# Queries and keys of heads 0 and 1 as two pairs of seven products ahead of the attention, parked in DRAM

## The chip, the cores and the metric

One core of a Trainium2 chip runs the kernel. The metric is device time in microseconds (us) of one execution. The kernel before was timed three times: 1097.13, 1096.53 and 1094.05 us, median 1096.53.

Every engine of the core runs its own instructions in its own order: TensorE (PE) multiplies, VectorE (DVE) and ScalarE (ACT) do elementwise work, GpSimd (POOL) and SyncE (SP) issue DMAs, and GpSimd also adds.

## What is computed

One block over 1024 tokens of width 1024. An adaLN-modulated RMSNorm gives `h`; one wide product `h @ w_in` gives everything else. The part that matters here is the gated linear attention:

```
q, k, v, z_gla, ra_f, ra_b, u, vs, z_gmlp, m_gla, m_gmlp = split(h @ w_in)
log_a = maximum(log_sigmoid(ra @ alpha_w + alpha_b) / 16, -1.25)      # per direction
b = cumsum(log_a) within chunks of 64 tokens
q_t, k_t, k_end = q * exp(b), k * exp(-b), k * exp(b_last - b)
attn = where(mask, q_t @ k_t.T, 0)
state = exp(b_last) * state + k_end.T @ v          # from chunk to chunk
o = attn @ v + q_t @ state                         # forward and backward, added
y_gla = (rmsnorm_per_head(o) * gla_norm_g * silu(z_gla)) @ w_br_gla
y_gmlp = (gelu(u) * spatial_gate(vs) * silu(z_gmlp)) @ w_br_gmlp
out = rmsnorm(x + gate * ((sigmoid(m_gla)*y_gla + sigmoid(m_gmlp)*y_gmlp) @ w_out))
```

There are 4 heads; a head's query and key have 128 columns each, its value 256.

## The kernel before

**Products.** Every fp32 matrix is split into a high part (rounded to fp32r) and a low part (the rest): `split_w` (L171) casts on ScalarE and subtracts on VectorE. One product of two matrices is then three matmuls: high by high, high by low, low by high. All activations lie with channels on partitions.

**Two ways to a block of columns.** A block is 128 columns of `w_in` over 1024 tokens.
- *Dense*: `dense_fm` (L185) and `fm_half` (L965) run 2 halves of 512 tokens by 8 slices of the inner dimension by 3 matmuls, 48 matmuls of 128x512 for a block.
- *Pair*: `pair` (L602) computes two blocks at once by seven products instead of eight, each `prod` (L580) of 12 matmuls of 128x512, 84 for two blocks where dense takes 96. It needs sums of the weights, which GpSimd makes (L610, L611, L612, L617), and sums of the results, which VectorE makes (L629 to L643), and it works on sums of `h` (`TS`) that are held while the pairs run.

**Stages.** First `h`, the values of heads 0 and 1 and the spatial gate. Then the pairs, one after another: `pair_m` (tanh of the merge gates, to DRAM), `pair_uz` (gMLP), `pair_z` (the gate of the attention, to DRAM `z_d`); the last is `pair_z(3)`. Around the end of the pairs stands `dense_q(0)`, and the transposes `low_rank` (L767) that make `RT`, the input of the decays.

**Attention.** 16 units (4 heads by 4: backward halves 1 and 0, forward halves 0 and 1). In `gla_unit` a *decay chain* runs for one unit: the decay product on TensorE (L793), Abs, Exp and Ln on ScalarE, two steps and a scan on VectorE, two Exp, and the products with `q` and `k`, of which `b` (L821) is the last. Then the *scores* (L830) can start. `front_a` of unit n+2 is emitted behind `front_b` (scores) of unit n+1, so that the decay product of the next unit directly follows the scores of this one on TensorE. Between the attention's small matmuls stands a *filler*: the list `jobs`, a generator that gives out dense work in steps of 12 matmuls of 128x512 (or 24 of 128x256 for values). `QUOTA` says how many steps are emitted per unit. The jobs before are key of head 0, query and key of head 1, value of head 2, query and key of head 2, value of head 3, query and key of head 3, and the blocks of `y_gmlp` (operand `gg`, loaded from DRAM by `load_gg`).

**End.** The last filler blocks, the product with `w_br_gla` (operand `GO`, loaded as `gf` from `g_d` and split to `gh`, `gl`), and the output projection.

**Order.** Each engine runs its instructions in the order in which the scheduler of the framework has put them, with a simulated timeline in mind; it moves instructions of independent work past each other within the limits of the buffers. SyncE's queue holds the weight loads. GpSimd's queue holds the DRAM writes of the pairs and the loads of `v`, `z` and, on a changed kernel, of `q` and `k`.

Of the kernel before, what the change touches and what calls it, by code (L numbers as in the profile page):

```python
# [9 lines left out]
F32 = mybir.dt.float32  # L10
F32R = mybir.dt.float32r
I8 = mybir.dt.int8
AF = mybir.ActivationFunctionType
ALU = mybir.AluOpType
# [3 lines left out]
P = 128  # L18
D = 1024
T = 1024  # L20
KC = D // P
NT = T // P
# [9 lines left out]
FB_Q, FB_K, FB_Z, FB_U, FB_ZG, FB_MA, FB_MB, FB_YA, FB_YB = 0, 4, 8, 16, 24, 32, 40, 48, 56  # L32
# [12 lines left out]
def hybrid_block_kernel(ctx: ExitStack, tc: tile.TileContext, x, wf, wt, wada, wgate, wvr, wst, alpha, abias,  # L45
                        pcols, prows, out):
    nc = tc.nc
    V, S, G, TE = nc.vector, nc.scalar, nc.gpsimd, nc.tensor
# [17 lines left out]
    def dram(name, shape, dtype=F32):  # L66
        return dr.tile(shape, dtype, tag=name, name=name)
# [6 lines left out]
    tb_d = dram("tb_d", [KC, P, T])  # L74
    z_d = dram("z_d", [KC, P, T])
    gate_d = dram("gate_d", [2, 512])
    b12_d = dram("b12_d", [4, P, 1024])

    v_d = [dram(f"v{n}_d", [HEADS, 2, P, 4 * 256]) for n in "hl"]
# [11 lines left out]
    def pm():  # L91
        return ps.tile([P, 512], F32, tag="m", bufs=2, name=nm("pm"))

    def po_():
        return ps.tile([P, 512], F32, tag="o", bufs=2, name=nm("po"))
# [5 lines left out]
    ident = cp.tile([P, P], F32, name="ident")  # L101
# [7 lines left out]
    ones = cp.tile([P, P], F32, name="ones")  # L109
# [5 lines left out]
    ra = cp.tile([P, NT, 32], F32, name="ra")  # L115


    def ht(shape, dtype, name):
        return hp.tile(shape, dtype, tag="h", bufs=30, name=nm(name))

    def w4(shape, dtype, name):
        return hp.tile(shape, dtype, tag="w", bufs=13, name=nm(name))

    def w2(shape, dtype, name):
        return hp.tile(shape, dtype, tag="s", bufs=18, name=nm(name))
# [32 lines left out]
    H = Act("h")  # L158
# [26 lines left out]
    def dense_fm(b, x, evac):  # L185

        hi, lo = fm_weights(b)
        for half in range(2):
            acc = pd()
            for k in range(KC):  # L190
                TE.matmul(acc, lhsT=hi[:, k, :], rhs=x.hi(k, half), start=(k == 0), stop=False)
                TE.matmul(acc, lhsT=hi[:, k, :], rhs=x.lo(k, half), start=False, stop=False)
                TE.matmul(acc, lhsT=lo[:, k, :], rhs=x.hi(k, half), start=False, stop=(k == KC - 1))
            evac(half, acc)
# [43 lines left out]
    for b in range(2):  # L238
        pc = pd()
        sl = slice(b * 512, b * 512 + 512)  # L240
# [307 lines left out]
    TOKENS = (4, 5, 6, 7, 0, 1, 2, 3)  # L548
# [11 lines left out]
    def v_weights(h, new):  # L560
        pieces = []
        for j in range(2):
            w = stage(wt[WV + 2 * (h - 1) + j])
            hi, lo = new([P, 4, HV], F32R, "tvh"), new([P, 4, HV], F32R, "tvl")
            split_w(w, flat(hi), flat(lo))
            for k in range(4):
                pieces.append((hi[:, k, :], lo[:, k, :]))
        return pieces
# [77 lines left out]
    def pair_m(b0, d, i):  # L646

        def ev(b, half, acc):
            m = w2([P, 512], F32, "m")
            S.activation(m, acc, AF.Tanh, scale=0.5)  # L650
            G.dma_start(d[2 * i + b, :, half * 512:half * 512 + 512], m)
        pair(b0 + 2 * i, b0 + 2 * i + 1, ev)
# [22 lines left out]
    def pair_z(i):  # L675

        def ev(b, half, acc):
            z = w2([P, 512], F32, "z")
            last_tanh[0] = S.activation(z, acc, AF.Tanh, scale=0.5)
            V.scalar_tensor_tensor(out=z, in0=z, scalar=1.0, in1=acc, op0=ALU.add, op1=ALU.mult)  # L680
            G.dma_start(z_d[2 * i + b, :, half * 512:half * 512 + 512], z)
        pair(FB_Z + 2 * i, FB_Z + 2 * i + 1, ev)

    last_tanh = [None]

    def low_rank_weights():

        ST = w4([P, T], F32R, "ST")
        sa, sr = ht([P, 1024], F32, "sa"), ht([P, 1024], F32R, "sr")
        G.memset(sa, 0.0)  # L690
        for r in range(3):
            G.dma_start(sa[r * 32:r * 32 + 16, 0:512], alpha[0])
            G.dma_start(sa[r * 32 + 16:r * 32 + 32, 512:1024], alpha[1])
        G.dma_start(sa[96:98, :], abias.partition_broadcast(2))
        S.copy(sr, sa)
        S.copy(ST[0:64, :], sr[0:64, :].bitcast(F32))
        V.tensor_tensor(out=sa[64:128, :], in0=sa[64:128, :], in1=sr[64:128, :].bitcast(F32), op=ALU.subtract)
        S.copy(ST[64:96, :], sa[64:96, :])
        S.activation(sa[96:128, :], sa[96:128, :], AF.Copy, scale=ident[96:128, 97:98])
        V.scalar_tensor_tensor(out=ST[96:128, :], in0=sr[96:128, :].bitcast(F32), scalar=ident[96:128, 96:97],  # L700
                               in1=sa[96:128, :], op0=ALU.mult, op1=ALU.add)
        return ST

    pair_m(FB_MB, tb_d, 0)
    pair_m(FB_MB, tb_d, 1)
    pair_uz(0)
# [8 lines left out]
    pair_m(FB_MA, ta_d, 2)  # L715
    pair_z(1)
    pair_m(FB_MA, ta_d, 3)
    pair_z(2)
    ST = low_rank_weights()
    pair_z(3)  # L720

    with tc.issue_after(last_tanh[0].ins):
# [8 lines left out]
    q_t = [None] * HEADS  # L731
    k_t = [None] * HEADS
    z_t = [[None, None] for _ in range(HEADS)]

    def dense_q(h):
        q_t[h] = ht([P, T], F32, "q")

        def ev(half, acc):
            S.activation(q_t[h][:, half * 512:half * 512 + 512], acc, AF.Copy, scale=float(P) ** -0.5)
        dense_fm(FB_Q + h, H, ev)  # L740

    def dense_k(h):
        k_t[h] = ht([P, T], F32, "k")

        def ev(half, acc):
            S.copy(k_t[h][:, half * 512:half * 512 + 512], acc)
        dense_fm(FB_K + h, H, ev)

    def load_z(h):
        for j in range(2):  # L750
            zt = z_t[h][j] = ht([P, T], F32, "zg")
            G.dma_start(zt, z_d[2 * h + j])

    RT = w4([P, T], F32R, "RT")

    V.tensor_copy(RT[96:128, :].rearrange("p (a b) -> p a b", b=P), ones[96:128].unsqueeze(1).broadcast_to([32, 8, P]))


    r3 = ht([P, NT, 3, 32], F32, "r3")
    for t in range(NT):  # L760
        V.tensor_copy(r3[:, t], ra[:, t, :].unsqueeze(1).broadcast_to([P, 3, 32]))

    def low_rank(half):
        sl = slice(half * 512, half * 512 + 512)
        pr = po_()
        for i in range(4):
            TE.transpose(pr[0:96, i * P:(i + 1) * P], r3[:, half * 4 + i].rearrange("p a b -> p (a b)"), ident)  # L767
        S.copy(RT[0:96, sl], pr[0:96])
        V.tensor_tensor(out=RT[32:64, sl], in0=pr[32:64], in1=RT[32:64, sl].bitcast(F32), op=ALU.subtract)

    v_t = {}

# [6 lines left out]
    V.memset(smask, 1.0)  # L779
    V.memset(smask.rearrange("p (c k) -> p c k", k=C)[:, :, 0:1], 0.0)  # L780

    dense_q(0)
    low_rank(1)
    low_rank(0)
    load_v(0, 1)
    load_v(0, 0)

# [189 lines left out]
    def ev_q(h):  # L977
        def ev(half, acc):
            S.activation(q_t[h][:, half * 512:half * 512 + 512], acc, AF.Copy, scale=float(P) ** -0.5)
        return ev  # L980

    def ev_k(h):
        def ev(half, acc):
            S.copy(k_t[h][:, half * 512:half * 512 + 512], acc)
        return ev
# [10 lines left out]
    def prep_qk(h, isk):  # L996
        (k_t if isk else q_t)[h] = ht([P, T], F32, "qk")
        return fm_weights((FB_K if isk else FB_Q) + h)

    def run_fm(x, evac, halves=(1, 0)):  # L1000
        def run(w):
            for half in halves:
                yield from fm_half(x, w, half, evac)
        return run

    def run_v(h):
        def run(pieces):
            for t in TOKENS:
                acc = pd()[:, 0:HV]
                v_steps(acc, pieces, t)  # L1010
                v_out(h, t, acc)
                yield
        return run
# [24 lines left out]
    def gg_second():  # L1038
        load_gg(1)
        return held["yb"]  # L1040

    jobs = [(lambda: prep_qk(0, True), run_fm(H, ev_k(0))),
            (lambda: prep_qk(1, False), run_fm(H, ev_q(1))),
            (lambda: prep_qk(1, True), run_fm(H, ev_k(1))),
            (lambda: v_weights(2, w4), run_v(2)),
            (lambda: prep_qk(2, False), run_fm(H, ev_q(2))),
            (lambda: prep_qk(2, True), run_fm(H, ev_k(2))),
            (lambda: v_weights(3, w4), run_v(3)),
# [23 lines left out]

    order = [(h, u) for h in range(HEADS) for u in range(4)]

    QUOTA = (4,) * 14 + (3, 3)
    load_z(0)
    dense(4)
    front_a(*order[0])
# [6 lines left out]
    for n, (h, u) in enumerate(order):  # L1085
        nxt = order[n + 1] if n + 1 < len(order) else None
        if u == 0 and h > 0:
            load_z(h)
        if u == 3 and h + 1 < HEADS:
            load_v(h + 1, 0)  # L1090
        if u == 1 and h + 1 < HEADS:
            load_v(h + 1, 1)
        last = order[n - 1] if n and SEQ[order[n - 1][1]][0] else None
        if last:
            norm(*last)
        dense(1)
        step(h, u, 0)
        dense(1)
        if last:
            output(*last)  # L1100
        step(h, u, 1)
        dense(QUOTA[n] - 3)
        if nxt:
            front_b(*nxt)
        step(h, u, 2)
        if n + 2 < len(order):
            front_a(*order[n + 2])
        dense(1)
        step(h, u, 3)
        if nxt:  # L1110
            front_c(*nxt)
# [226 lines left out]
```

## Time and profile before

| | us |
|---|---|
| median of three runs | 1096.53 |
| profiled execution | 1096.96 |
| its span | 1095.3 |
| outside the span | 1.7 |
| TensorE busy | 1057.6 |
| VectorE busy | 641.1 |
| ScalarE busy | 412.1 |
| GpSimd busy | 276.1 |

A row of the timeline gives start, busy time, engine, line, operation and, in brackets, the idle time before it with what ended it. Matmuls are pipelined: a 128x512 matmul is shown as 0.39 to 0.40 us long, while the next one starts earlier; its cost to the engine is the distance of starts. In windows the columns are the stretch, its length, and busy us (with the number of instructions) of PE, PEld, DVE, ACT and POOL; then the clock granted to TensorE as a share of full speed, the share of the DMA engines that was busy, and GB/s. A row of the waits gives who waited for whom, us in total, times, longest.

### The profile page before, as it was taken

Reading aid. Unit: us, or ns where it says so; the run is one execution under the profiler, and the core shown is the slowest. Engines: PE = TensorE matmul, PEld = TensorE weight load, DVE = VectorE, ACT = ScalarE, POOL = GpSimd, SP = SyncE. Lnnn points to the kernel's source line nnn. Section 1 sums busy time; section 2 is a strip of 40 time slices with the busy share of each in tenths; the row PEclk is TensorE's granted clock in tenths of the full one; section 3 lists DMA queues with packets and bytes.
Section 4 is the critical chain, followed back from the end, with each engine's and each line's share of the span. In section 5 each row is a group of like instructions: output and inputs, shape, how many; then the busy total and the mean of one; then the engine's idle time right before and its main releaser. Section 6 shows DMA issues by size and latency. Waiting matters only on the chain.

```text
span 1095.3 us, 14011 instructions
## 1 busy us (share of the span) xinstructions
PE 1057.6 (97%) x5292; PEld 892.7 (82%) x5292; DVE 641.1 (59%) x960; ACT 412.1 (38%) x721; POOL 276.1 (25%) x304
## 2 busy tenths in 40 slices
PE   6899999999999999999999999999999989995997
PEld 4688899888888888878888898998888778884886
DVE  5777497346547464664554576658767556345522
ACT  4454334233333323343323546457254253111322
POOL 2311203424334352453402001102011010005510
PEclk9899999999999999999999999999999999997999
DMA  9532276233233323223348024347344385235012
GB/s 362 215 128 70 104 253 221 79 118 104 106 116 106 125 97 119 103 104 135 135 145 291 17 83 149 131 140 250 128 161 136 127 294 183 83 119 193 1 58 96
DMA packets 57032, 152.80 MB, mean 140 GB/s; under 512 B 7457, under 2 KB 15649, under 8 KB 56966
## 3 DMA queue, kind: packets, MB, share of 16 engines
q1 hardware_dynamic: 42198, 102.42, 27.0%
q0 software_dynamic: 14768, 49.50, 12.5%
q8 instruction: 41, 0.67, 0.3%
q14 instruction: 25, 0.20, 0.1%
HBM read 108.90 MB, written 43.00 MB: 139 GB/s over the span
## 4 chain that ended last, share of the span: by engine, by line
PE 81%; DVE 5%; issue 5%; DMA 4%; ACT 2%; POOL 1%; SPq 0%; POOLq 0%; ACTq 0%; DVEq 0%
PE pd L210 5%; PE pd L211 5%; PE po L589 4%; PE po L587 4%; PE po L588 4%; PE pd L209 4%; PE pd L969 4%; PE pd L970 4%; PE pd L971 4%; PE pk L587 3%; PE pk L589 3%; PE pk L588 3%; PE pd L587 3%; PE pd L588 3%; PE pd L589 3%
## 5 line engine op out<-in xcount | busy, mean ns | idle before, releaser
L543 PE MATMUL pd<-tvh,hh 128*128 128x256 f32 (+1 forms) x256 | 75.0, 293 | 0.0
L544 PE MATMUL pd<-tvl,hh 128*128 128x256 f32 (+1 forms) x256 | 73.8, 288 | 0.0
L545 PE MATMUL pd<-tvh,hl 128*128 128x256 f32 (+1 forms) x256 | 73.4, 287 | 0.0
L219 POOL TENSOR_TENSOR r<-ms,nhalf 128x1 f32<-128x1 f32 (+1 forms) x24 | 21.6, 900 | 193.1 <-DVE ms L218 184.5
L589 PE MATMUL pd<-hh,al 128*128 128x512 f32 x160 | 62.5, 390 | 0.0
L587 PE MATMUL pd<-hh,ah 128*128 128x512 f32 x160 | 62.3, 390 | 0.0
L588 PE MATMUL pd<-hl,ah 128*128 128x512 f32 x160 | 62.3, 389 | 0.0
L209 PE MATMUL pd<-th,mh 128*128 128x512 f32 x120 | 47.0, 403 | 7.8 <-ACT th L173 7.8
L969 PE MATMUL pd<-ggh,wh 128*128 128x512 f32 x128 | 51.8, 405 | 1.8 <-ACT wh L173 1.8
L210 PE MATMUL pd<-tl,mh 128*128 128x512 f32 x120 | 48.3, 403 | 3.5 <-DVE tl L174 3.5
L971 PE MATMUL pd<-ggh,wl 128*128 128x512 f32 x128 | 51.6, 405 | 0.0
L970 PE MATMUL pd<-ggl,wh 128*128 128x512 f32 x128 | 51.1, 399 | 0.0
L174 DVE TENSOR_TENSOR al<-wa,ah 128x1024 fp32r<-128x1024 f32 x20 | 31.4, 1571 | 32.7 <-PE po L588 30.8
L1167 PE MATMUL pd<-gl,wh 128*128 128x512 f32 x128 | 49.8, 389 | 0.0
L1166 PE MATMUL pd<-gh,wl 128*128 128x512 f32 x128 | 49.6, 389 | 0.0
L1165 PE MATMUL pd<-gh,wh 128*128 128x512 f32 x128 | 49.6, 389 | 0.0
L610 POOL TENSOR_TENSOR wsum<-wb 128x512 f32<-128x512 f32 x20 | 25.8, 1288 | 94.2 <-DMA wb<-in_wf 69.7
L544 PEld LDWEIGHTS pd<-tvl,hh 128*128 128x128 f32 x256 | 48.7, 190 | 0.9 <-issue 0.5
L543 PEld LDWEIGHTS pd<-tvh,hh 128*128 128x128 f32 x256 | 48.7, 190 | 0.8 <-issue 0.5
L545 PEld LDWEIGHTS pd<-tvh,hl 128*128 128x128 f32 x256 | 48.7, 190 | 0.0
L211 PE MATMUL pd<-th,ml 128*128 128x512 f32 x120 | 48.0, 400 | 0.0
L174 DVE TENSOR_TENSOR wl<-ws,wh 128x1024 fp32r<-128x1024 f32 x24 | 29.3, 1220 | 30.0 <-ACT wh L173 28.8
(318 smaller groups left out, 3108.0 us busy)
## 6 DMA issues: line engine op xcount, KB each, us to landing
ws<-in_wf SPq DMA_DIRECT2D x24, 512.0 KB, 5.3
ws<-in_wt SPq DMA_DIRECT2D x22, 512.0 KB, 4.8
wa<-in_wf SPq DMA_DIRECT2D x20, 512.0 KB, 3.6
wb<-in_wf SPq DMA_DIRECT2D x20, 512.0 KB, 4.6
wa<-in_wada SPq DMA_DIRECT2D x16, 512.0 KB, 9.3
xn<-in_x SPq DMA_DIRECT2D x8, 512.0 KB, 7.4
sg_d<-sg POOLq DMA_DIRECT2D x16, 256.0 KB, 3.1
wg<-in_wgate SPq DMA_DIRECT2D x16, 256.0 KB, 5.3
```

What stands on the lines that cost most here:

```text
L209: TE.matmul(acc, lhsT=xh, rhs=hi[:, k % 2, :], start=(k == 0), stop=False)
L210: TE.matmul(acc, lhsT=xh, rhs=lo[:, k % 2, :], start=False, stop=False)
L211: return TE.matmul(acc, lhsT=xl, rhs=hi[:, k % 2, :], start=False, stop=(k == KC - 1))
L543: TE.matmul(acc, lhsT=H.hi_t(k, t), rhs=hi, start=(k == 0), stop=False)
L544: TE.matmul(acc, lhsT=H.hi_t(k, t), rhs=lo, start=False, stop=False)
L545: i = TE.matmul(acc, lhsT=H.lo_t(k, t), rhs=hi, start=False, stop=(k == KC - 1))
L587: TE.matmul(acc, lhsT=a, rhs=xh(k), start=(first and k == 0), stop=False, skip_group_check=not first)
L588: TE.matmul(acc, lhsT=a, rhs=xl(k), start=False, stop=False, skip_group_check=not first)
L589: TE.matmul(acc, lhsT=b, rhs=xh(k), start=False, stop=(k == 3), skip_group_check=not first)
L969: TE.matmul(acc, lhsT=hi, rhs=x.hi(k, half), start=(k == 0), stop=False)
L970: TE.matmul(acc, lhsT=hi, rhs=x.lo(k, half), start=False, stop=False)
L971: TE.matmul(acc, lhsT=lo, rhs=x.hi(k, half), start=False, stop=(k == KC - 1))
```

## The change

`q` and `k` of heads 0 and 1 are no longer computed densely. Two new pairs, over blocks `FB_Q`, `FB_Q+1` and `FB_K`, `FB_K+1`, compute them among the other pairs and write them to new DRAM tensors `q_d` and `k_d`. `load_qk(h)` brings them back by GpSimd's queue, head 0 ahead of the attention and head 1 in its second unit. The transposes for `RT` move ahead of `pair_z(3)` and use another PSUM buffer. The first three filler jobs are gone, so the list opens with the values of head 2, and the quota falls from 62 to 52 steps.

```diff
+    def pair_qk(b0, d, scale):
+        def ev(b, half, acc):
+            r = w2([P, 512], F32, "z")
+            S.activation(r, acc, AF.Copy, scale=scale)
+            G.dma_start(d[b, :, half * 512:half * 512 + 512], r)
+        pair(b0, b0 + 1, ev)
...
     pair_m(FB_MA, ta_d, 3)
+    pair_qk(FB_Q, q_d, float(P) ** -0.5)
     pair_z(2)
     ST = low_rank_weights()
+    pair_qk(FB_K, k_d, 1.0)
+    RT = w4([P, T], F32R, "RT")
+    low_rank_inputs(RT)
     pair_z(3)
...
-    def dense_q(h):
-    def dense_k(h):
...
+    def load_qk(h):
+        for l, d in ((q_t, q_d), (k_t, k_d)):
+            l[h] = ht([P, T], F32, "qk")
+            for half in (1, 0):
+                sl = slice(half * 512, half * 512 + 512)
+                G.dma_start(l[h][:, sl], d[h, :, sl])
...
-    dense_q(0)
-    low_rank(1)
-    low_rank(0)
+    load_qk(0)
...
-    jobs = [(lambda: prep_qk(0, True), run_fm(H, ev_k(0))),
-            (lambda: prep_qk(1, False), run_fm(H, ev_q(1))),
-            (lambda: prep_qk(1, True), run_fm(H, ev_k(1))),
-            (lambda: v_weights(2, w4), run_v(2)),
+    jobs = [(lambda: v_weights(2, w4), run_v(2, (0, 1, 2, 3, 4, 5, 6, 7))),
...
-    QUOTA = (4,) * 14 + (3, 3)
+    QUOTA = (3, 3, 4, 3) * 4
...
+        if (h, u) == (0, 1):
+            load_qk(1)
```

`low_rank_inputs` holds the lines of the old `low_rank`, with `pm()` in place of `po_()`.

On TensorE the end of the pairs is, before, the last product of `pair_z(3)` (L587 to L589), the last matmuls of head 0's query (L191 to L193), the transposes (L767) and the key of head 0 (L969 to L971):

```order
L589 MATMUL pk_4537<-hh_106,fl_4474 128x512
L193 MATMUL pd_4645<-hh_106,wl_4616 128x512
L191 MATMUL pd_4645<-hh_106,wh_4615 128x512
L192 MATMUL pd_4645<-hl_107,wh_4615 128x512
L193 MATMUL pd_4645<-hh_106,wl_4616 128x512
L767 MATMUL po_4671<-ident,r_800_4600 96x128 x4
L969 MATMUL pd_4704<-hh_4590,wh_4700 128x512
```

After, head 2's values (L545 to L547, 128x256) stand between the products of `pair_z(3)` (L589 to L591) on TensorE:

```order
L547 MATMUL pd_4962<-tvh_4914,hl_99 128x256
L545 MATMUL pd_4962<-tvh_4914,hh_98 128x256
L546 MATMUL pd_4962<-tvl_4915,hh_98 128x256
L547 MATMUL pd_4962<-tvh_4914,hl_99 128x256
L589 MATMUL pk_4830<-t0h_1539,sh_4757 128x512
L590 MATMUL pk_4830<-t0l_1540,sh_4757 128x512
L591 MATMUL pk_4830<-t0h_1539,sl_4758 128x512
```

The dense query and the transposes have left this place, and the filler now begins among the pairs.

In head 3, the unit of TensorE that ends with the scores of the first forward half closes before like this; `ggh`, `ggl` with L969 to L971 are filler, L848 to L850 state products, L830 the next scores:

```order
L848 MATMUL pk_7145<-vh_6550,keh_7045 128x256
L849 MATMUL pk_7145<-vl_6551,keh_7045 128x256
L850 MATMUL pk_7145<-vh_6550,kel_7046 128x256
L969 MATMUL pd_7251<-ggh_6581,wh_7076 128x512
L970 MATMUL pd_7251<-ggl_6582,wh_7076 128x512
L971 MATMUL pd_7251<-ggh_6581,wl_7077 128x512
...
L969 MATMUL pd_7251<-ggh_6588,wh_7076 128x512
L970 MATMUL pd_7251<-ggl_6589,wh_7076 128x512
L971 MATMUL pd_7251<-ggh_6588,wl_7077 128x512
L830 MATMUL pm_7264<-qh_7168,b_7159 128x128 x4
```

And the same end of that unit on TensorE after (state products are L852 to L854, scores L834, transposes of the output L950):

```order
L950 MATMUL po_7194<-ident,op_7007 128x128 x2
L950 MATMUL po_7201<-ident,op_7007 128x128 x2
L852 MATMUL pk_7224<-vh_6699,keh_7137 128x256
L853 MATMUL pk_7224<-vl_6700,keh_7137 128x256
L854 MATMUL pk_7224<-vh_6699,kel_7138 128x256
L852 MATMUL pk_7268<-vh_6699,keh_7137 128x256
L853 MATMUL pk_7268<-vl_6700,keh_7137 128x256
L854 MATMUL pk_7268<-vh_6699,kel_7138 128x256
L852 MATMUL pk_7296<-vh_6975,keh_7279 128x256
L853 MATMUL pk_7296<-vl_6976,keh_7279 128x256
L854 MATMUL pk_7296<-vh_6975,kel_7280 128x256
L834 MATMUL pm_7324<-qh_7247,b_7238 128x128 x4
```

In this unit 24 filler matmuls stand where there were 48, and 12 state products where there were 6.

ScalarE in the same unit after: the decay chain's Abs (L799), the cast of `gf` (L175), four normalisations of the head's output (L941), then Exp and Ln (L800, L801):

```order
L799 ACTIVATE e_7232<-pm_7230 128x512
L175 CAST gh_7737<-gf_7739 128x1024
L941 ACTIVATE op_7007<-op_7007,r_7146 128x256 x4
L800 ACTIVATE e_7232<-e_7232 128x512
L801 ACTIVATE e_7232<-e_7232 128x512
```

The cast of `gf` stood one unit later before.

## Rows read from the trace of the kernel before

**Rows 1.** The page: span, busy time by engine, granted TensorE clock in 40 slices.

```profile
span 1095.3 us, 14011 instructions
...
PE 1057.6 (97%) x5292; PEld 892.7 (82%) x5292; DVE 641.1 (59%) x960; ACT 412.1 (38%) x721; POOL 276.1 (25%) x304
...
PEclk9899999999999999999999999999999999997999
```

**Rows 2.** The page: the chain that ended last, shares by engine.

```profile
PE 81%; DVE 5%; issue 5%; DMA 4%; ACT 2%; POOL 1%; SPq 0%; POOLq 0%; ACTq 0%; DVEq 0%
```

**Rows 3.** Windows by stage: us, then PE, PEld, DVE, ACT, POOL busy, PEclk, DMA.

```profile
400.00:588.00 188.00, 186.86 (x819) 153.23 (x819) 108.26 (x131) 65.95 (x89) 73.67 (x86) 1.00 0.37 130
601.00:887.00 286.00, 279.64 (x1648) 245.49 (x1646) 189.58 (x334) 139.81 (x311) 29.52 (x47) 0.99 0.41 142
985.00:1095.00 110.00, 92.65 (x412) 75.97 (x411) 43.72 (x53) 26.11 (x51) 37.38 (x23) 0.93 0.23 89
```

**Rows 4.** Timeline, TensorE: start us, busy us, engine, line, operation, count.

```profile
564.72 0.40 PE L191 MATMUL pd<-hh,wh 128*128 128x512 f32 x1
...
565.86 0.39 PE L193 MATMUL pd<-hh,wl 128*128 128x512 f32 x1
```

**Rows 5.** Timeline, SyncE queue: first weight load of two successive pairs.

```profile
474.76 0.33 SPq L606 DMA_DIRECT2D wa<-in_wf  x1
...
493.73 0.33 SPq L606 DMA_DIRECT2D wa<-in_wf  x1
```

**Rows 6.** Groups by form, VectorE, 400 to 600: busy us, mean ns, idle before.

```profile
L174 DVE TENSOR_TENSOR al<-wa,ah 128x1024 fp32r<-128x1024 f32 x8 | 12.6, 1579 | 9.2 <-PE po L588 9.0 <-ACT ah L173 0.2
L174 DVE TENSOR_TENSOR bl<-wb,bh 128x1024 fp32r<-128x1024 f32 x8 | 9.8, 1226 | 8.5 <-ACT bh L173 8.5
```

**Rows 7.** Waits of TensorE, 400 to 600: us, times, longest.

```profile
PE pk L587 <- DVE u L643: 1.1, 1, 1.1
```

**Rows 8.** Waits of TensorE, 600 to 900.

```profile
PE pm L830 <- DVE b L821: 2.6, 1, 2.6
PE pd L969 <- ACT wh L173: 1.8, 1, 1.8
PE po L848 <- DVE zg L948: 0.7, 1, 0.7
```

**Rows 9.** Windows around the longest wait of the attention.

```profile
858.00:862.00 4.00, 4.00 (x13) 3.15 (x12) 2.83 (x5) 0.62 (x1) 0.50 (x1) 0.62 0.59 197
```

**Rows 10.** Chain of waits, 838 to 860: start us, us, what.

```profile
842.50 4.42 DMA gf<-g_d
...
846.95 1.05 ACT gh L173
...
854.46 1.21 DVE gl L174
...
856.33 1.16 PE pm L830 x8
```

**Rows 11.** Timeline, TensorE: start of the decay product of three units.

```profile
757.50 0.48 PE L793 MATMUL pm<-RT,ST 128*128 128x512 f32 x1
...
825.96 0.48 PE L793 MATMUL pm<-RT,ST 128*128 128x512 f32 x1
...
840.07 0.48 PE L793 MATMUL pm<-RT,ST 128*128 128x512 f32 x1
```

**Rows 12.** Timeline, VectorE: last step of two units' decay chain.

```profile
772.86 0.68 DVE L821 TENSOR_TENSOR b<-b,qk 128x512 f32<-128x512 f32 x1
...
855.59 0.68 DVE L821 TENSOR_TENSOR b<-b,qk 128x512 f32<-128x512 f32 x1
```

**Rows 13.** One line's instructions, ScalarE L937: count: min/median/max ns.

```profile
L937 ACT ACTIVATE op<-op,r x32: 492/495/511, 667.4 to 891.8; 128x256 f32<-128x256 f32 x32
```

**Rows 14.** One line's instructions, VectorE L948.

```profile
L948 DVE SCALAR_TENSOR_TENSOR zg<-po,gn,zg x16: 723/744/752, 672.4 to 897.3; 128x512 f32<-128x512 f32 x16
```

**Rows 15.** Timeline, TensorE: start of the output projection.

```profile
993.72 1.65 PE L209 MATMUL pd<-th,mh 128*128 128x512 f32 x3 [7.83 <-ACT th L173]
```

More of the change, by code (lines that the diff above doesn't have):

```diff
@@ L76, in hybrid_block_kernel @@
     gate_d = dram("gate_d", [2, 512])
+    q_d = dram("q_d", [2, P, T])
+    k_d = dram("k_d", [2, P, T])
     b12_d = dram("b12_d", [4, P, 1024])
@@ L702, in low_rank_weights, with low_rank_inputs @@
         return ST
+    def low_rank_inputs(RT):
+        V.tensor_copy(RT[96:128, :].rearrange("p (a b) -> p a b", b=P),
+                      ones[96:128].unsqueeze(1).broadcast_to([32, 8, P]))
+        r3 = ht([P, NT, 3, 32], F32, "r3")
+        for t in range(NT):
+            V.tensor_copy(r3[:, t], ra[:, t, :].unsqueeze(1).broadcast_to([P, 3, 32]))
+        for half in (1, 0):
+            sl = slice(half * 512, half * 512 + 512)
+            pr = pm()
+            for i in range(4):
+                TE.transpose(pr[0:96, i * P:(i + 1) * P], r3[:, half * 4 + i].rearrange("p a b -> p (a b)"), ident)
+            S.copy(RT[0:96, sl], pr[0:96])
+            V.tensor_tensor(out=RT[32:64, sl], in0=pr[32:64], in1=RT[32:64, sl].bitcast(F32), op=ALU.subtract)
     pair_m(FB_MB, tb_d, 0)
@@ L733, in hybrid_block_kernel @@
     z_t = [[None, None] for _ in range(HEADS)]
-    def dense_q(h):
[L736 to L740, printed above, removed]
-    def dense_k(h):
[L743 to L747, printed above, removed]
+    def load_qk(h):
+        for l, d in ((q_t, q_d), (k_t, k_d)):
+            l[h] = ht([P, T], F32, "qk")
+            for half in (1, 0):
+                sl = slice(half * 512, half * 512 + 512)
+                G.dma_start(l[h][:, sl], d[h, :, sl])
     def load_z(h):
@@ L752, in load_z @@
             G.dma_start(zt, z_d[2 * h + j])
[L754 to L769, printed above, removed]
     v_t = {}
@@ L1004, in run_fm, with run_v @@
         return run
-    def run_v(h):
+    def run_v(h, tokens=TOKENS):
         def run(pieces):
-            for t in TOKENS:
+            for t in tokens:
                 acc = pd()[:, 0:HV]
```

## The prediction

> **What bounds the kernel now.** I read the page's busy shares first, then the chain that ended last, then windows by stage, and then the waits of TensorE. TensorE is busy for 1057.6 of 1095.3 us [rows 1] and holds 81% of the chain [rows 2]. The windows say where it is not: in the pairs it lacks 188.0 - 186.86 = 1.1 us, in the attention 286.0 - 279.64 = 6.4 us, and at the output projection 110.0 - 92.65 = 17.4 us [rows 3]. So in the pairs and in the attention any TensorE work that is taken away shortens the end one for one, as long as the other engines still deliver within the shorter time. Whether they do is the question of this case, and it has to be asked unit by unit: over the whole attention VectorE is busy 189.6 of 286 us and ScalarE 139.8 [rows 3], but in one unit they work as a chain, one behind the other.
>
> **What goes from TensorE.** Busy time per matmul misleads here: 0.40 us is shown, while five starts lie 565.86 - 564.72 = 1.14 us apart, 0.228 us each [rows 4]. Four blocks went densely through 4 x 48 = 192 matmuls; two pairs take 2 x 84 = 168. That is 24 x 0.228 = 5.5 us less. A whole pair as a check: 84 x 0.228 = 19.2 us, and the first weight loads of two successive pairs lie 493.73 - 474.76 = 19.0 us apart [rows 5], so a pair runs at TensorE's rate.
>
> The Trainium skill ("TensorE: Matmul & The Clock Gate", section Back-to-back issue gap) gives 131 ns per matmul of 512 columns in a sustained stream; by that the 24 would be worth 3.1 us. The row differs, 0.228 us, and decides.
>
> **What the pairs add elsewhere.** Each new pair brings GpSimd sums, three splits of 128x1024 and one of half that, five VectorE adds of the results, one more ScalarE copy, and four evictions with DMA writes. In the pairs VectorE is busy 108.3 of 188 us, ScalarE 66.0, GpSimd 73.7 [rows 3], and this is the work that already stands beside pairs of the same length; two more of them hide it in the same way. The one wait in nine or so pairs was 1.1 us, on a VectorE add [rows 7]; I cost a new pair at nothing, and at 1.1 us each, 2.2 in all, if neither is hidden. The DMA traffic is 2 MB written and 2 MB read, behind a DMA share of 0.37 in this stretch [rows 3]. The loads of head 0 are issued before the attention's first scores with a whole pair between, so they cost nothing; if that cover fell away, one landing of a similar load, 4.4 us [rows 10], is the bound. Moving the transposes and V2 into the last pair changes only the order of TensorE's work: 0.
>
> The Trainium skill ("SBUF — State Buffer", section SBUF: two separate sides) says that a VectorE instruction with two SBUF inputs and a GpSimd instruction that reads SBUF exclude each other, one blocking the other for the whole instruction. The trace bears out a part: the same split takes 1579 ns where the pair's sums run on GpSimd beside it and 1226 ns where they don't [rows 6]. That is 0.35 us per split, which stays hidden under TensorE as long as VectorE has 80 us to spare in 188.
>
> **What the attention loses.** The three dense jobs (12 steps) go and the quota falls by ten, so the units get thinner. I take from the order how much TensorE work stands between two scores, and from the trace how long the decay chain takes.
>
> The unit that I fear is the one in head 3 that ends with the scores of its first forward half. Before, its decay product started at 825.96 and the next at 840.07 [rows 11], 14.1 us, with no listed wait. After, it has 24 filler matmuls fewer (-5.5 us) and six state products of half the width more (+0.7): 9.3 us, of which about 8.5 lie between decay product and scores. Its chain is the long one: the order puts the cast of `gf` behind Abs, and four normalisations behind the cast. The unit that had this cast before started at 840.07 and its last VectorE step ended at 855.59 + 0.68 = 856.27 [rows 11, 12], 16.2 us. In it, the load took 4.42 us, the cast began only at 846.95, 6.9 us after the decay product, and the VectorE half of the split, 1.21 us, stands in the chain as well [rows 10]. In the changed unit the load is issued about 1.4 us before the decay product (it waits for a slot that TensorE frees just ahead of the scores), so the cast starts some 3 us after it, 3.9 us sooner; but four normalisations of 0.495 us [rows 13] and two gate products of 0.744 us [rows 14] enter: 16.2 - 3.9 + 2.0 + 1.5 = 15.8 us. The wait is 15.8 - 8.5 = 7.3 us. Bounds: 5.5, if the load has landed when the cast's turn comes, and 7.7 with the whole 16.2. I take 7.
>
> A wait of that length also costs clock. After the 2.6 us wait before these scores [rows 8] the granted clock of the next 4 us was 0.62 [rows 9], which is 2.4 GHz for a quarter of it and 1.2 GHz for the rest: 4 x 0.38 = 1.5 us lost. After the longer wait ahead of the output projection, 7.83 us [rows 15], the stretch to the end ran at 0.93 on the mean. I add 2 us for the 7 us wait.
>
> The other units: one in head 1 has 12.2 us of work where chains of 10.7 to 12.6 are usual, 0.5; one in the same head loads `gg` behind the last values of head 3, a load and a split ahead of the first filler that needs it, 0 to 4, I take 1.5; one in head 2 stays as it was, 0.4. In return the end of the attention fills: the 1.8 us wait for a weight split and the 0.7 us one for a gate product [rows 8] stood where filler had run low, and the 2.6 us wait with its 1.5 us of clock goes, since the cast has left that unit, whose work of 14.1 us covers a chain without it. I leave 1.0 us of all these.
>
> **Sum.** The attention loses now 6.4 us of waits [rows 3] and 1.5 of clock: 7.9. After: 7 + 2 + 0.5 + 1.5 + 0.4 + 1.0 = 12.4, so 4.5 more. Against it stand 5.5 us less work. Net -1.0 us. The output projection's waits hang on loads that stand in the same order on SyncE's queue, 0. The profiled execution took 1096.96 us (span 1095.3 and 1.7 outside), 0.4 above the median; 1096.96 - 1.0 = 1096.0, and on the median's scale 1095.5 us.
>
> **Rivals.**
> *The full gain.* The chains get shorter where the units get thinner, because part of a chain's time was queueing behind evictions that TensorE's own dense work produced. For it: VectorE is idle for a third of the attention [rows 3], and a wait of 2.6 us was all that the 16.2 us chain cost before [rows 8]. Against it: cast, normalisations and gate products stand in the chain by order, not by chance. Then the thin unit waits about as long as the longest before (2.6 + 1.5), the rest gains its 2.5 at the end: -5.5 - 2.5 = -8.0, 1088.5 us; with the attention's loss just as before, 1091.0.
> *The chain decides every thinned unit.* Chains stay as long as they were even in units with more cover. One at 757.50 ended at 772.86 + 0.68 = 773.54, 16.0 us [rows 11, 12]; the unit in that place now has 14.2 us between scores, so it waits 2.5 with the 0.7 from scores to decay product. With it the last unit keeps its 2.6 + 1.5. That is 6.6 on top of my forecast: 1102.1 us. It decides once TensorE's work between scores falls below some 16 us, which it does in eleven of the fifteen such stretches. For it: chains of 16 us where a cast stands in them. Against: most others show no wait at 14 to 16 us of work.
> *The port.* If VectorE and GpSimd block each other more in two more pairs, each pays the 1.1 us wait [rows 7]: +2.2, 1097.7 us.
>
> **How the numbers follow.** About 0.3%, 3.3 us, is what a measurement of this kernel can tell from no change: faster means under 1093.2, slower over 1099.8. I give the forecast 0.42, the full gain 0.31, the chain in every unit 0.22, the port 0.05. The forecast's own spread (the thin unit 5.5 to 7.7, `gg` 0 to 4, clock 1.5 to 3) stays within 3 us. Faster 0.31, same 0.46, slower 0.23. The range reaches to the two rivals, 1088 to 1102.5; the forecast's own is 1092.5 to 1098.5.
>
> **What would show it.** TensorE's matmuls number 24 fewer of 128x512, and the pairs of Q and K run 19 us each with no wait beyond 1 us. The longest wait of the attention stands at the scores of head 3's first forward half, L834 behind VectorE L825, 5.5 to 7.7 us long, with a clock of about half for some microseconds behind it; ahead of it on ScalarE lie the cast of `gf` and four L941. The wait of 1.8 us for a weight split near the end of the attention is gone. I am wrong if that unit waits under 3 us (then the time is near 1089 to 1091), or if three or more units wait over 2 us each (then 1100 and above), or if TensorE waits for `q` or `k` at the first scores.

## The result and the profile after

The changed kernel took 1103.18 us (median of 4 runs, 1102.54 to 1104.45), the kernel before 1096.83 beside it: ratio 1.0065, 95% interval 1.0045 to 1.0084. It is slower by 6.4 us, just outside the range of 1088 to 1102.5, and on the side that I had given 0.23.

The page of the changed kernel: span, busy time by engine, and the granted clock in 40 slices.

```profile
span 1101.8 us, 14052 instructions
...
PE 1055.7 (96%) x5268; PEld 888.8 (81%) x5268; DVE 652.1 (59%) x974; ACT 415.6 (38%) x727; POOL 296.5 (27%) x328
...
PEclk9899999999999999999999999998999899997999
```

TensorE does less work in more time: 5268 matmuls against 5292 [rows 1], 24 fewer as counted, and the span is 6.5 us longer. The clock row shows two slices under 9 tenths more in the attention than [rows 1]. The windows of the changed attention (columns as in [rows 3]) say where:

```profile
700.00:750.00 50.00, 47.02 (x276) 40.22 (x275) 36.15 (x67) 27.83 (x66) 4.70 (x9) 1.00 0.47 157
750.00:800.00 50.00, 47.95 (x239) 40.18 (x240) 38.03 (x61) 26.27 (x54) 10.07 (x15) 0.93 0.56 191
800.00:850.00 50.00, 48.70 (x268) 41.40 (x266) 33.55 (x60) 26.76 (x63) 7.03 (x11) 1.00 0.40 127
850.00:900.00 50.00, 43.92 (x211) 36.99 (x212) 29.84 (x53) 14.65 (x35) 5.97 (x10) 0.90 0.47 164
```

From 600 to 900 TensorE lacks 12.6 us of busy time (0.2 in the first 100 us, the rest in these rows), and the clock of 0.93 and 0.90 takes another 3.5 and 5.0. That is 21.1 us, where the kernel before lost 6.4 [rows 3] and 1.5 [rows 9] in its attention. So 13.2 us more were lost and 5.5 us of work saved: 7.7 later. The trace agrees:

```profile
1001.14 1.65 PE L211 MATMUL pd<-th,mh 128*128 128x512 f32 x3 [8.10 <-ACT th L175]
```

The output projection starts at 1001.14, before at 993.72 [rows 15], 7.4 us later. Its own wait is 8.1 us against 7.8. From that start to the end of the span the changed kernel takes 100.7 us, the kernel before 101.6, and so 6.5 us remain at the end.

The waits of TensorE from 600 to 900, columns as in [rows 8]:

```profile
PE pk L852 <- DVE s L871: 4.7, 2, 4.1
PE pd L973 <- ACT wh L175: 2.3, 1, 2.3
PE pk L854 <- DVE kel L848: 1.9, 2, 1.6
PE pd L975 <- DVE wl L176: 1.3, 1, 1.3
PE po L852 <- ACT po L935: 1.3, 2, 0.8
```

Two places make nearly all of this. The first is behind the last scores of head 1, where the filler turns from the values of head 3 to the `y_gmlp` blocks. TensorE there, from one unit's scores to the next:

```profile
738.34 1.05 PE L834 MATMUL pm<-qh,b 128*128 128x128 f32 x8
...
750.71 0.79 PE L973 MATMUL pd<-ggh,wh 128*128 128x512 f32 x1 [2.30 <-ACT wh L175]
...
753.27 0.79 PE L975 MATMUL pd<-ggh,wl 128*128 128x512 f32 x1 [1.34 <-DVE wl L176]
...
756.85 0.63 PE L974 MATMUL pd<-ggl,wh 128*128 128x512 f32 x1
757.28 0.53 PE L975 MATMUL pd<-ggh,wl 128*128 128x512 f32 x1
757.65 0.40 PE L973 MATMUL pd<-ggh,wh 128*128 128x512 f32 x1
...
761.88 0.39 PE L834 MATMUL pm<-qh,b 128*128 128x128 f32 x2
```

From 738.34 to 761.88 are 23.5 us for a unit in which the order places 12 to 13.5 us of work. From 739 to 751 TensorE has nothing but the small attention matmuls, with two waits for ScalarE's evictions (0.85 and 0.41 us); then it waits 2.30 us for the high part of the first weight and 1.34 us for its low part, and until 757.28 its matmuls run at 0.43 us distance, the 1.2 GHz level, instead of 0.23. These waits and the clock make 8.4 us; the rest of the unit's excess is shown as busy time, between short matmuls whose starts lie further apart. ScalarE's queue in that stretch:

```profile
742.86 1.03 ACT L175 CAST ggh<-ggf 128x1024 fp32r<-128x1024 f32 x1
...
748.67 1.05 ACT L175 CAST ggh<-ggf 128x1024 fp32r<-128x1024 f32 x1
749.60 1.06 ACT L175 CAST wh<-ws 128x1024 fp32r<-128x1024 f32 x1
```

The cast of the first weight (749.60) stands behind four casts of `gg`, the first of them at 742.86, with the evictions of the heads' outputs and the decay chain's Exp and Ln between them. The loads are not late: those of the first half of `gg` are issued from 722.60 to 726.7 and land at most 5.4 us later. ScalarE then sits idle for 2.11 us (to 740.45) and 0.64 us (to 741.84) at an eviction and a cast of the scores, which wait for TensorE and VectorE, and the casts of `gg` stand behind these in its queue. The other place is the unit in head 3 that I had feared, first in the chain of waits and then on TensorE:

```profile
840.77 4.87 DMA gf<-g_d
...
845.74 1.05 ACT gh L175
846.78 1.61 ACT op L941 x4
...
852.02 1.30 DVE zg L952 x2
...
853.84 0.58 PE pk L852
```

```profile
840.95 1.05 PE L834 MATMUL pm<-qh,b 128*128 128x128 f32 x8
841.75 0.48 PE L797 MATMUL pm<-RT,ST 128*128 128x512 f32 x1
...
858.44 2.08 PE L834 MATMUL pm<-qh,b 128*128 128x128 f32 x8
```

The decay product starts at 841.75, its scores at 858.44: the chain runs through the load of `gf`, its cast, the four normalisations and the two gate products, and takes 16.7 us. The unit lasts 17.5 us; the next, at low clock for its first part, ends with the scores at 875.30 and lasts 16.9.

Nothing else moved much. In the pairs, the first weight loads of two successive pairs, and all that TensorE waits for from 400 to 624:

```profile
492.96 0.33 SPq L608 DMA_DIRECT2D wa<-in_wf  x1
...
512.10 0.33 SPq L608 DMA_DIRECT2D wa<-in_wf  x1
```

```profile
PE pk L589 <- DVE u L645: 1.3, 2, 0.8
```

19.1 us per pair, 19.0 before [rows 5], and 1.3 us of waits in eleven pairs against 1.1 [rows 7]. No wait stands at the first scores for `q` or `k`.

### The profile page after: what moved, and what is told of

Same layout as the page of the kernel before. It is cut to its first block, busy times and chain, and to the rows that moved or that the text cites. A ratio compares the mean times of both kernels' runs of the same rounds, so it can differ in the third digit from the quotient of the medians.

```text
span 1101.8 us, 14052 instructions
## 1 busy us (share of the span) xinstructions
PE 1055.7 (96%) x5268; PEld 888.8 (81%) x5268; DVE 652.1 (59%) x974; ACT 415.6 (38%) x727; POOL 296.5 (27%) x328
## 4 chain that ended last, share of the span: by engine, by line
PE 87%; DVE 5%; ACT 3%; DMA 2%; issue 2%; POOL 1%; SPq 0%; POOLq 0%; ACTq 0%; DVEq 0%
PE po L591 5%; PE po L590 5%; PE po L589 5%; PE pd L212 4%; PE pd L213 4%; PE pd L211 4%; PE pd L975 4%; PE pd L973 4%; PE pd L974 4%; PE pk L589 4%; PE pk L591 3%; PE pk L590 3%; PE pd L591 3%; PE pd L589 3%; PE pd L590 3%; PE pd L546 3%
## 5 line engine op out<-in xcount | busy, mean ns | idle before, releaser
L545 PE MATMUL pd<-tvh,hh 128*128 128x256 f32 (+1 forms) x256 | 74.3, 291 | 0.0
L547 PE MATMUL pd<-tvh,hl 128*128 128x256 f32 (+1 forms) x256 | 74.0, 289 | 0.0
L589 PE MATMUL pd<-hh,ah 128*128 128x512 f32 x176 | 68.6, 390 | 0.0
L590 PE MATMUL pd<-hl,ah 128*128 128x512 f32 x176 | 68.5, 389 | 0.0
L591 PE MATMUL pd<-hh,al 128*128 128x512 f32 x176 | 68.5, 389 | 0.0
L612 POOL TENSOR_TENSOR wsum<-wb 128x512 f32<-128x512 f32 x22 | 28.9, 1312 | 98.1 <-DMA wb<-in_wf 81.2
L545 PEld LDWEIGHTS pd<-tvh,hh 128*128 128x128 f32 x256 | 48.7, 190 | 0.9 <-issue 0.5
L547 PEld LDWEIGHTS pd<-tvh,hl 128*128 128x128 f32 x256 | 48.8, 190 | 0.3
L175 ACT CAST sh<-wsum 128x1024 fp32r<-128x1024 f32 x22 | 23.2, 1053 | 60.0 <-PE po L591 36.5
```

The lines of the kernel that those rows point to most:

```text
L545: TE.matmul(acc, lhsT=H.hi_t(k, t), rhs=hi, start=(k == 0), stop=False)
L547: i = TE.matmul(acc, lhsT=H.lo_t(k, t), rhs=hi, start=False, stop=(k == KC - 1))
L589: TE.matmul(acc, lhsT=a, rhs=xh(k), start=(first and k == 0), stop=False, skip_group_check=not first)
L590: TE.matmul(acc, lhsT=a, rhs=xl(k), start=False, stop=False, skip_group_check=not first)
L591: TE.matmul(acc, lhsT=b, rhs=xh(k), start=False, stop=(k == 3), skip_group_check=not first)
```

## The experiments

**Theories.** A: the time goes into the attention, where units with less filler than before can no longer cover the decay chains and the splits that ScalarE and VectorE owe, and where the waits cost clock as well. B: the detour of `q` and `k` costs, through the pairs' extra work, GpSimd's queue or DRAM. Each ratio is against the kernel before, run on the same chip.

**Old quota on the changed kernel.**

```diff
-    QUOTA = (3, 3, 4, 3) * 4
+    QUOTA = (4,) * 14 + (3, 3)
```

> The changed kernel with the old quota of 62 filler steps in place of 52, all else as changed: q and k still go through pairs and DRAM. Theory A (the loss sits where the attention has run short of filler): the wait for the first gg weights in head 1 (about 10 us with its slow clock) and the wait in head 3 ahead of the scores (about 11 us) shrink, while the filler runs out in the last unit, which then loses 5 to 8; 1094 to 1099 us. Theory B (the detour of q and k through GpSimd's queue and DRAM, or the pairs themselves, costs the time): nothing of that is undone, 1102 to 1104 us.

1095.8 us, ratio 1.0006 (0.9997 to 1.0016). One line takes the loss back, with both pairs and the detour in place. Windows of this kernel's attention up to 850 and behind it, and its longest wait:

```profile
600.00:850.00 250.00, 250.00 (x1475) 221.09 (x1474) 169.50 (x291) 123.07 (x261) 38.16 (x66) 1.00 0.51 174
850.00:900.00 50.00, 43.81 (x240) 35.08 (x238) 36.60 (x65) 27.66 (x69) 5.84 (x8) 1.00 0.61 213
```

```profile
902.10 0.51 PE L1169 MATMUL pd<-gh,wl 128*128 128x512 f32 x1 [3.47 <-DVE wl L176]
```

The waits in head 1 and ahead of 850 are gone (250.00 of 250), while the queries and keys of heads 0 and 1 come from DRAM all the same: theory B, which had 1102 to 1104 us, falls here. The first matmul with `gg` comes at 734.60, two units earlier in the order than in the changed kernel: the quota has moved the job's start as well. The 5.5 us of saved work still do not show in the time. They are lost at the end, where the filler has run out: 6.2 us up to 900, the clock staying at 1.00, and a wait of 3.5 us for the low part of a weight of the product with `w_br_gla`, with a clock of 0.79 from 900 to 908, around its end and behind it.

**Only the split of `gf` later.** On the changed kernel:

```diff
...
-                split_w(flat(g), flat(hi), flat(lo))
+                with tc.issue_after(last_exp[0].ins), tc.issue_after(last_b[0].ins):
+                    split_w(flat(g), flat(hi), flat(lo))
```

(`last_exp` and `last_b`, set in lines that are not shown, are the last Exp and the last product of the last decay chain.)

> The changed kernel with one order forced: on ScalarE and VectorE the split of gf is queued behind the last decay chain. Theory A with the chain as I read it: the cast and its wait (843.5 to 846.8) and the VectorE half (1.2 us) leave the chain of head 3, 16.6 us becomes about 12, against 9 us of TensorE work; the wait there falls from 6.3 us to about 3 and most of the slow clock goes with it: 1096 to 1099 us. Theory B: no change, 1102 to 1104 us.

1099.19 us, ratio 1.0034 (1.0021 to 1.0046). The scores at either end of the unit in head 3:

```profile
839.88 1.05 PE L836 MATMUL pm<-qh,b 128*128 128x128 f32 x8
...
852.65 0.58 PE L836 MATMUL pm<-qh,b 128*128 128x128 f32 x1
```

12.8 us instead of 17.5: 4.7 us come back in that unit, so the place of the split is worth about half of the loss there. Most of the slow clock stays, 0.93 over 850 to 900 in place of 0.90, and the time is 0.2 us above what A expected. The waits at `gg` are untouched (2.3 and 1.8 us in this run).

**Half of the change.** Queries by a pair, keys dense:

```diff
-    pair_qk(FB_K, k_d, 1.0)
...
-        for l, d in ((q_t, q_d), (k_t, k_d)):
+        for l, d in ((q_t, q_d),):
...
-    jobs = [(lambda: v_weights(2, w4), run_v(2, (0, 1, 2, 3, 4, 5, 6, 7))),
+    jobs = [(lambda: prep_qk(0, True), run_fm(H, ev_k(0))),
+            (lambda: prep_qk(1, True), run_fm(H, ev_k(1))),
+            (lambda: v_weights(2, w4), run_v(2, (0, 1, 2, 3, 4, 5, 6, 7))),
...
-    QUOTA = (3, 3, 4, 3) * 4
+    QUOTA = (4,) * 12 + (3,) * 4
```

> Half of the change: queries of heads 0 and 1 by a pair and DRAM, keys of heads 0 and 1 dense in the filler again, quota 60. TensorE works 2.7 us less than before and 2.7 more than with the whole change, and the attention has eight more filler steps. Theory A: the gg wait goes since that unit has 76 filler matmuls again; one thin unit stays in head 2 and one at the end; 1093 to 1097 us. Theory B: half the detour, half the loss, 1099 to 1101 us.

1093.25 us, ratio 0.998 (0.9971 to 0.9988): 0.2% faster than the kernel before, and by the ratios 0.9% faster than the changed one. Its windows:

```profile
700.00:750.00 50.00, 50.00 (x306) 44.79 (x306) 34.38 (x61) 25.44 (x57) 4.47 (x7) 1.00 0.53 182
750.00:800.00 50.00, 47.38 (x247) 40.31 (x246) 36.62 (x62) 22.85 (x46) 9.32 (x16) 0.97 0.53 162
```

From 700 to 750, where the whole change lost 3.0 us, nothing is lost; 2.6 us and some clock go in one thin unit of head 2.

**Split of `gf` later and another quota.** The edit of the second experiment and

```diff
-    QUOTA = (3, 3, 4, 3) * 4
+    QUOTA = (3,) * 7 + (4,) * 8 + (3,)
```

> The changed kernel with the split of gf behind the last decay chain and the quota (3,)*7 + (4,)*8 + (3,), which spends filler from the tail in the later units. Theory A: no unit of the last two heads has under 13.7 us of work, so the waits of head 3 go; the gg start keeps 3 to 8 us of its loss: 1090 to 1096 us. Theory B: 1102 to 1104 us.

1095.15 us, ratio 0.9996 (0.9984 to 1.0008). Within what A expected; the wait for the first `gg` weight stays, 2.4 us, in the same unit behind the last scores of head 1, though that unit has a quota of 4 again; the seven before it have 3.

**Weights ahead of `gg`.**

```diff
     def gg_first():
+        w = [fm_weights(FB_YB + j) for j in range(2)]
         load_gg(0)
-        return [fm_weights(FB_YB + j) for j in range(2)]
+        return w
```

> The changed kernel with one edit: the weights of the first two y_gmlp blocks are loaded and split ahead of the first half of gg. Theory A1 (in head 1 TensorE waits because the cast of the first weight stands on ScalarE behind four casts of gg and the evictions): the wait of 2.3 and the one of 1.3 us behind it go, and with them the slow clock, 4 to 6 us: 1097 to 1099. Theory A2 (it is not that cast but the whole of the splits, two tiles of weight or gg, that ScalarE and VectorE owe in a stretch without filler): the wait only moves to another operand, 1101 to 1104 us.

1102.51 us, ratio 1.0052 (1.0039 to 1.0066). TensorE at the first filler matmul of that stretch:

```profile
750.46 0.98 PE L973 MATMUL pd<-ggh,wh 128*128 128x512 f32 x2 [2.88 <-ACT ggh L175]
```

The wait has moved from the weight to the first `gg`, 2.9 us in place of 2.3 and 1.3, and the ratio is within the interval of the changed kernel's. A2 holds against A1: the wait is not tied to that one cast, it moves to another of the splits in a stretch without filler.

**The kernel before with the thin quota alone.**

```diff
-    QUOTA = (4,) * 14 + (3, 3)
+    QUOTA = (3, 3, 4, 3) * 4
```

> The kernel before with only the quota lowered from 62 to 52 steps; dense queries and keys, no pairs of q and k. Theory A (thin units cost, whatever thins them): several units fall to 8 to 12 us of TensorE work where chains take 11 to 16, so 8 to 16 us of waits and slow clock with no work saved: 1103 to 1112 us. Theory B (the detour of q and k costs): no change, 1094 to 1098 us.

1104.82 us, ratio 1.0077 (1.0063 to 1.009). The kernel before gets as slow as the changed one without any of its pairs. Its longest waits among the attention, and three of its windows:

```profile
PE pk L848 <- ACT keh L843: 3.0, 2, 2.2
PE pm L840 <- DVE atb L897: 2.0, 1, 2.0
PE pd L969 <- ACT wh L173: 1.9, 1, 1.9
PE pm L830 <- DVE b L821: 1.8, 3, 1.4
```

```profile
600.00:700.00 100.00, 98.02 (x609) 88.26 (x608) 62.79 (x115) 49.17 (x111) 7.03 (x11) 0.98 0.27 92
700.00:750.00 50.00, 47.80 (x340) 44.34 (x339) 35.15 (x68) 28.06 (x71) 5.87 (x9) 0.97 0.56 166
800.00:850.00 50.00, 44.45 (x228) 37.06 (x228) 40.31 (x69) 24.48 (x55) 6.57 (x11) 0.97 0.40 143
```

The places differ (2.0, 2.2 and 5.5 us are lost in these windows, where [rows 3] shows 6.4 for the whole), the kind is the same: the decay chain, its casts, and a filler operand.

**Half of the change with the late split.** The kernel of the half change, the edit of the second experiment, and

```diff
-    QUOTA = (4,) * 12 + (3,) * 4
+    QUOTA = (4,) * 16
```

> Only the pair of queries, keys of heads 0 and 1 dense in the filler, the split of gf behind the last decay chain, quota (4,)*16. Only one unit, in head 2, has under 13.7 us of work (9.1). Theory A: one wait of 3 to 5 us with its clock stays; 1090 to 1093 us, below the half change with the early gf. Theory B: as the half change, 1093 us.

1095.85 us, ratio 0.9992 (0.9981 to 1.0003). A miss: no faster than the half change by itself (0.9971 to 0.9988); the intervals overlap, so that it is slower is not shown. Besides the thin unit of head 2, TensorE lost time at the head of the product with `w_br_gla`:

```profile
892.48 0.51 PE L1172 MATMUL pd<-gh,wh 128*128 128x512 f32 x1 [2.49 <-ACT wh L175]
```

```profile
890.00:900.00 10.00, 6.84 (x18) 5.34 (x19) 4.36 (x5) 7.12 (x17) 1.01 (x1) 0.66 0.87 307
```

The first weights of the next stage come late for TensorE, 2.5 us, at a clock of 0.66 over 10 us. Two things were changed at once here; the kernel with the old quota, where the split was not moved, has its 3.5 us wait in the same place, so the filler spent in the units is the likelier cause.

**Both pairs, late split, quota of 61.** The edit of the second experiment and

```diff
-    QUOTA = (3, 3, 4, 3) * 4
+    QUOTA = (4, 4, 4, 4, 4, 4, 4, 3, 4, 4, 4, 3, 4, 4, 4, 3)
```

> Both pairs, the split of gf behind the last decay chain, quota of 61 steps. No unit waits in heads 0 and 1; the filler has run out by the last unit (9.3 us of work) and nothing stands between the last steps. Theory A: 5.5 us of work less, no wait up to head 2, some 8 lost in the last unit and behind it: 1092 to 1096 us. Theory B: 1102 us.

1093.98 us, ratio 0.9979 (0.9969 to 0.999). With the half change, the fastest that I found, 0.2% under the kernel before; it keeps all of the change's pairs. Two windows:

```profile
600.00:800.00 200.00, 200.00 (x1211) 178.33 (x1210) 133.31 (x228) 99.66 (x209) 30.56 (x53) 1.00 0.51 176
850.00:900.00 50.00, 43.73 (x237) 35.19 (x237) 36.53 (x62) 26.07 (x60) 5.57 (x8) 1.00 0.60 200
```

Up to 800 nothing is lost, where the changed kernel lost 5.0 us and 3.5 of clock. 6.3 us go from 850 to 900, where the filler is at an end.

## Why the prediction was wrong

- **Work taken from TensorE, 5.5 us:** right, 24 matmuls fewer and the pairs at 19.1 us each.
- **The pairs, the detour, the moved transposes at nothing:** right; 1.3 us of waits in the pairs against 1.1, none at the first scores. The rival of the port is out as the cause with that, 0.2 us more where it had 2.2. But I had misread [rows 6]: their 1579 ns is a mean over unlike cases (median 1226 ns, longest 2206). In the changed kernel six of ten such splits take 1.21 to 1.23 us, and the longest 2.21, with an add on GpSimd beside it. The Trainium skill ("SBUF — State Buffer", section SBUF: two separate sides) has one of the two engines blocked outright. The trace agrees with that in single instructions: here are such a split, an elementwise step behind it that takes 0.69 us elsewhere, and the wait that follows on TensorE, for the step that stands next in VectorE's queue; so this much of the 1.3 us is the port.

```profile
483.46 2.21 DVE L176 TENSOR_TENSOR al<-wa,ah 128x1024 fp32r<-128x1024 f32 x1
...
486.97 2.27 DVE L682 SCALAR_TENSOR_TENSOR z<-z,p 128x512 f32<-128x512 f32 x1 [0.70 <-ACT z L681]
...
489.89 0.50 PE L589 MATMUL pk<-t0h,sh 128*128 128x512 f32 x1 [0.81 <-DVE u L645]
```

- **The thin unit of head 3, a wait of 7 us:** right in place and mechanism. Measured 6.3 us (4.09, 0.62 and 1.60), chain 16.7 against my 15.8. TensorE waited not at the scores but at the state products just ahead of them, whose operands stand in VectorE's and ScalarE's queues among the steps of the same chain.
- **Its clock, 2 us:** too small by 3. The 0.90 of 850 to 900 is 5.0 us. I had priced it by [rows 9], after a wait of 2.6 us; here it stayed low longer, at 0.50, the 1.2 GHz level throughout, from 858 to 862:

```profile
850.00:858.00 8.00, 1.94 (x6) 1.38 (x6) 7.17 (x14) 1.84 (x4) 1.14 (x2) 0.70 0.17 66
858.00:862.00 4.00, 3.98 (x13) 3.32 (x14) 3.42 (x7) 0.78 (x1) 1.08 (x2) 0.50 0.81 298
862.00:866.00 4.00, 4.00 (x18) 3.27 (x17) 2.17 (x4) 2.65 (x5) 0.00 (x0) 0.83 0.61 220
```

- **The start of `gg` in head 1, 0 to 4 us, taken as 1.5:** this is the step that failed. Waits of 0.85, 0.41, 2.30 and 1.34 make 4.9 us, and the clock of 0.93 another 3.5: 8.4 us. I had counted a load and one split as the delay. The loads had landed long before; what TensorE waited for is ScalarE's queue, in which four casts of `gg`, the cast of the first weight, the evictions and the steps of the decay chain stand behind each other, and I had not added these up. Nor had I put a clock price on this wait. (The 0.85 us stand ahead of the first cast of `gg`; they belong to the thin unit and not to its splits.)
- **The one in head 2, 0.4, and 0.5 for another in head 1:** 0.9 us of listed waits and some more (the unit of head 2 lasts 12.9 us, 805.83 - 792.97, for about 10 of work).
- **The end of the attention, 1.0 left:** 0.2, the waits of [rows 8] there are gone.

Sum: 12.4 us forecast, 21.1 measured. The start of `gg` is 6.9 over, head 3 2.3, all of it clock; the end of the attention 0.8 under. Added up the other way, the waits are 12.6 us where I had 10.4, and the clock 8.5 where I had 2 at one place: so most of the 8.7 us between forecast and measurement is clock. The rival that came out, slower by thin units, stood near at 1102.1, but by luck: it priced one wait of 2.5 us at a long chain and kept an old one at the end, though its condition held in eleven stretches, and neither of the two is in the trace. The loss is in two places, head 3, which the forecast itself had, and the *splits* of the next job in a unit without filler, which makes the largest error. That the thinning alone does this is shown by the two kernels that change only the quota, one in each direction: 1.0065 to 1.0006, and 1 to 1.0077. Whether the wait at `gg` hangs on the filler of its own unit or on the unit in which the quota lets the job start is not separated: with a quota of 4 in that unit and 3 before it the wait stayed, and with 4 up to there the job starts elsewhere. What part the clock has by itself was read from the windows only; no kernel was run that has these waits in these places without the clock falling.

## What to carry to other kernels

Work that fills the gaps of a latency chain can be worth more than its own time: three dense blocks (3 x 48 x 0.228 = 33 us) left the filler here, 5.5 us of work were saved, and 13.2 us of waits and clock came in their place. When a change takes filler, give the rest out again, unit by unit: add up what each in-order helper engine has to do in the thinnest stretch (evictions, casts of the next job's operands, the chain itself), in the order of its queue, and compare it to the work that remains on the bound engine. Here the stretch in which a job's first operands are split needed its filler; and filler spent early was missed at the end, where the kernel with the old quota lost what it had saved. No kernel here came out more than about 0.2% under the kernel before.

## What the runs showed of the hardware that was not expected

Idle time of the same amount costs clock or doesn't, and these runs give no rule for it. In the kernel with 61 steps 6.3 us were lost from 850 to 900, in waits of at most 0.85 us, at a granted clock of 1.00. In the changed kernel 2.05 us of idle time from 750 to 800 went with 0.93, after a stretch of short attention matmuls and waits. Nor does the bunching decide it: in the kernel with the old quota three waits from 870 to 876 (0.57, 1.35 and 0.49 us) went with 1.00, while in the half change three from 779 to 783 (1.25, 0.86 and 0.49 us) are all the idle time of a window at 0.97.

A VectorE instruction can take far longer than its mean: the same split of 128x1024 took 1.22 us or 2.21, and a step of 0.69 us took 2.27, with adds on GpSimd beside them.
